# Down products by column quarters, four early blocks of the second input product, shared banks and a new place for memory blocks in a two-block decoder kernel

## Chip, cores and metric

The kernel runs on one core of one Trainium2 chip. The metric is the device time of one execution in microseconds; smaller is better. The weights lie in HBM and are read once.

## What is computed

Two decoder blocks over 256 tokens of width 1024, in fp32. The first ends in a mixture of 32 experts, of which each token takes two; the kernel reads all experts' weights. The second has four mixers on slices of one input product, a cross attention to 256 memory rows and a feed-forward net.

```python
hid = jax.nn.silu(jnp.matmul(xb, w_g[e])) * jnp.matmul(xb, w_u[e])
return jnp.matmul(hid, w_d[e]) * wb[:, None]
...
proj = rms_norm_2(h, g_mix[l]) @ w_in[l]
ya = short_conv_mixer(pa, w_sconv[l])
yb = dilated_mixer(pb, cos, sin)
yc = forgetting_mixer(pc, b_forget[l])
yd = pool_mixer(pd, w_pool[l], pool_scale[l])
h = h + jnp.concatenate([ya, yb, yc, yd], axis=-1) @ w_out[l]
h = h + memory_cross_attention(rms_norm_2(h, g_xa[l]), rms_norm_2(mem, g_mem[l]), w_xq[l], w_xkv[l], w_xo[l])
h = h + conv_ffn(rms_norm_2(h, g_ffn[l]), w_up[l], w_ffconv[l], w_down[l])
```

## The kernel before

**Weights** come as tiles of 1 MiB ([128 x 2048] fp32) into a ring of 23 slots in SBUF. `build` (L561 to L622) writes the order of all loads as a list, `coming`; `pump` issues the next one from SP (`load_next`, L326) when a slot is free. Dense weights are used as blocks of half a tile. Most are split into a high part (ACT, L369) and a low part (DVE, L372), and a product is then three products, L461 to L463 (`mm3`: low by high, high by low, high by high). A block in the list `FULL`, or an early block of `wkv`, is not split and is multiplied in fp32.

**Experts** (`experts`, L1428): eight groups of four experts. The four experts of a group stand side by side in the array, 32 rows each. A group has 16 tiles of gate and up weights (L1544) and 8 tiles of down weights (`down`, L1515). A down tile holds one 128-row slice f of the hidden width and one half n of the columns for the four experts: four products of 512 columns. After the eight tiles a half's sum is copied out (ACT), brought back to token order by products with `back` (L1597, called y here) and added to xT. For the last group this is `back_half`, started after four and after eight down tiles; it also makes the high and low parts (`norm_high`, `norm_low`) of xT for the second block's input product.

**Memory blocks** are the 16 blocks of `w_xkv`: eight of keys (L472) and eight of values (L1399 in fp32). Four are multiplied in block 1, eight at group 6 (`MOE_AT`, `MOE_KV`), three behind the last down tile (`V_PLACE`, split), and one among the mixers. `AHEAD_OF_LAST` puts one of their tiles in front of the last four expert tiles in the list of loads.

**The second block's input product**, columns for queries and keys (`pq`) and for values (`pv`): four blocks of two k-slices each (`projN`, L502), each 12 products of 512 columns. Both are made in `mixers`, first `pq`, then `pv`.

**Output products** use `partT` (L489): for the first `k` outputs (128 columns each) the k-slices already known are multiplied, and once attention is there the rest. In block 1 two outputs are made in this way, in the mixers' output three (`MIX_PART`), in cross attention four. Each output has a PSUM bank of its own. When an output is finished, `residual` adds it to xT on DVE (L1649; L1114 in block 1) and makes the norm pieces of the next stage.

**Order of work.** Each engine works in program order. The program is written as a main line with coroutines: `spawn` starts one, each `tick` lets each go one step. `horizon` limits how far ahead weight blocks may be split. In the feed-forward net the last four down blocks are multiplied at the end, first for the one, then for the other half of the columns (`products`, L2079).

Of the kernel before, what the change touches and what calls it, by code (L numbers as in the profile page):

```python
# [14 lines left out]
OP = mybir.AluOpType  # L15
# [3 lines left out]
P = 128  # L19
# [27 lines left out]
AHEAD_OF_LAST = (1, 4)  # L47
MEM_AT = 12
FILL = 1
MOE_KV = 8  # L50
MOE_AT = 6
RANK = 4
V_PLACE = 3
MIX_PART = 3
# [4 lines left out]
KV_EARLY = sum(KV_PLACE.values()) + MOE_KV  # L59
# [82 lines left out]
def pack(x):  # L142
# [8 lines left out]
    def chan(v):  # L151
# [38 lines left out]
    pa = blocks_T(w2[:, :768]).reshape(P, 3, 2, 1024).transpose(0, 2, 1, 3).reshape(P, -1)  # L190
    w2 = chunks(
        blocks_N(w2[:, 768:1280]), blocks_N(np.concatenate([w2[:, 1280:1536], w2[:, 2048:2304]], 1)),
# [6 lines left out]
    we = np.concatenate([four(eg, KT, 1), four(eu, KT, 1), four(ed, 4, 2)], 1)  # L199
# [35 lines left out]
class Net:  # L235
# [20 lines left out]
    def bank(self):  # L256
        return self.t(self.ps, [P, 512], "ps")

# [88 lines left out]
    def queue(self, name, shapes):  # L347

        n = len(shapes)
        return [  # L350
            ((name, j // 2), j % 2, s, j % 2 == 1 or j == n - 1, (name == "wkv" and j < KV_EARLY) or (name, j) in FULL) for j, s in enumerate(shapes)
        ]
# [112 lines left out]
    def projT(self, out, w, h, ks, col=0, start=None, stop=None):  # L465

        for k in ks:
# [3 lines left out]
            if len(w) == 1:  # L471
                self.nc.tensor.matmul(out, w[0][:, k, c], h[2][:, k, :], start=a, stop=z)  # L472
            else:
                self.mm3(out, (w[0][:, k, c], w[1][:, k, c]), (h[0][:, k, :], h[1][:, k, :]), a, z)
# [14 lines left out]
    def partT(self, outs, h, first, rest):  # L489

        ws = []
        for o in outs:
            ws.append(self.next_block())
            self.projT(o, ws[-1][0], h, first, stop=False)
            yield None
        self.before_rest()
        for i, (o, (w, release)) in enumerate(zip(outs, ws)):
            self.projT(o, w, h, rest, start=False)
            release()
            yield i  # L500

    def projN(self, outs, h):  # L502

        for b in range(4):
            w, release = self.next_block()
            for j in range(2):
                k = 2 * b + j
                for tt in range(2):
                    s = slice(tt * P, tt * P + P)
                    if len(w) == 1:  # L510
                        self.nc.tensor.matmul(outs[tt][:], h[2][:, k, s], w[0][:, j, :], start=k == 0, stop=k == 7)
                    else:
                        self.mm3(
                            outs[tt][:], (h[0][:, k, s], h[1][:, k, s]), (w[0][:, j, :], w[1][:, j, :]), k == 0, k == 7
                        )
            release()
# [44 lines left out]
    def build(self):  # L561
# [35 lines left out]
        late = KV_EARLY + V_PLACE  # L597
# [1594 lines left out]
```

## Time and profile before

| | |
|---|---|
| median of 3 runs | 1049.95 us (1049.3 to 1051.71) |
| profiled execution, its own time | 1052.21 us |
| its span in the profile | 1050.40 us |
| mean granted TensorE clock | 0.925 |
| busy: PE, DVE, ACT | 907.5, 515.6, 344.0 us |
| read by DMA | 301.61 MB |

The span is the profiled part of one execution. "Idle before" in a row is the time for which that engine stood still ahead of the instruction, with what released it. The clock is a share of 2.4 GHz. Matmuls overlap: a row's duration is longer than the distance to the next start.

### The profile page before, as it was taken

Reading aid. Unit: us, or ns where it says so; the run is one execution under the profiler, and the core shown is the slowest. Engines: PE = TensorE matmul, PEld = TensorE weight load, DVE = VectorE, ACT = ScalarE, POOL = GpSimd, SP = SyncE. Lnnn points to the kernel's source line nnn. Section 1 sums busy time; section 2 is a strip of 40 time slices with the busy share of each in tenths; the row PEclk is TensorE's granted clock in tenths of the full one; section 3 lists DMA queues with packets and bytes.
Section 4 is the critical chain, followed back from the end, with each engine's and each line's share of the span. In section 5 each row is a group of like instructions: output and inputs, shape, how many; then the busy total and the mean of one; then the engine's idle time right before and its main releaser. Section 6 shows DMA issues by size and latency. Waiting matters only on the chain.

```text
span 1050.4 us, 14787 instructions
## 1 busy us (share of the span) xinstructions
PE 907.5 (86%) x5988; PEld 641.7 (61%) x5989; DVE 515.6 (49%) x1133; ACT 344.0 (33%) x614; POOL 1.3 (0%) x12
## 2 busy tenths in 40 slices
PE   6999989979776667576865986999999999999996
PEld 6659979834312204031322621688899899999995
DVE  7999968521110101001010021648576489888886
ACT  5326645311100001000000011564464466555553
POOL 0000000000000000000000000000000000000000
PEclk9999999999976968889789996999999999999999
DMA  9926556879999999999999999952364285552001
GB/s 370 386 79 240 175 187 212 336 301 426 426 427 427 427 426 426 426 427 427 427 427 425 428 426 427 426 189 88 120 223 181 83 363 179 195 185 97 1 1 41
DMA packets 44778, 301.61 MB, mean 287 GB/s; under 512 B 5024, under 2 KB 7456, under 8 KB 8864
## 3 DMA queue, kind: packets, MB, share of 16 engines
q1 hardware_dynamic: 44128, 300.01, 70.8%
q8 instruction: 49, 0.80, 0.3%
q10 hardware_dynamic: 576, 0.59, 0.2%
q14 instruction: 25, 0.20, 0.1%
HBM read 299.54 MB, written 1.05 MB: 286 GB/s over the span
## 4 chain that ended last, share of the span: by engine, by line
DMA 38%; PE 37%; DVE 2%; ACT 1%; issue 0%; SPq 0%; ACTq 0%; DVEq 0%
DMA slot<-in_we_dram 36%; PE ps L461 10%; PE ps L463 10%; PE ps L462 10%; DMA slot<-in_wkv_dram 2%; PE ps L1515 1%; PE ps L1544 1%; DVE slot L372 1%; PE ps L1995 1%; PE ps L1961 1%; PE ps L1597 0%; PE ps L1490 0%; PE ps L1581 0%; PE ps L1777 0%; PE ps L1774 0%
## 5 line engine op out<-in xcount | busy, mean ns | idle before, releaser
L461 PE MATMUL ps<-slot,slot 128*128 128x256 f32 (+1 forms) x1020 | 304.3, 298 | 0.4 <-DVE k L1836 0.4
L462 PE MATMUL ps<-slot,slot 128*128 128x256 f32 (+1 forms) x1020 | 296.8, 291 | 0.9 <-DVE slot L372 0.8
L463 PE MATMUL ps<-slot,slot 128*128 128x256 f32 (+1 forms) x1020 | 296.8, 291 | 0.3 <-DVE slot L372 0.2
L1544 PE MATMUL ps<-slot,k 128*32 128x512 f32 x1024 | 163.7, 748 | 81.0 <-DMA slot<-in_we_dram 74.7
L461 PEld LDWEIGHTS ps<-slot,slot 128*128 128x128 f32 x1020 | 195.9, 192 | 12.3 <-issue 7.0
L462 PEld LDWEIGHTS ps<-slot,slot 128*128 128x128 f32 x1020 | 196.0, 192 | 6.1 <-DVE slot L372 1.8
L372 DVE TENSOR_TENSOR slot<-slot,slot 128x1024 fp32r<-128x1024 f32 x159 | 191.9, 1218 | 13.5 <-ACT slot L369 13.5
L463 PEld LDWEIGHTS ps<-slot,slot 128*128 128x128 f32 x1020 | 195.9, 192 | 3.3 <-DVE slot L372 0.7
L369 ACT ACTIVATE slot<-slot 128x1024 fp32r<-128x1024 f32 x158 | 163.6, 1050 | 48.4 <-PE ps L463 38.6
L1544 PEld LDWEIGHTS ps<-slot,k 128*32 128x32 f32 x1024 | 26.7, 119 | 210.1 <-DMA slot<-in_we_dram 164.2
L1515 PE MATMUL ps<-slot,k 128*32 128x512 f32 x512 | 68.8, 667 | 25.9 <-DMA slot<-in_we_dram 20.0
L1583 DVE TENSOR_TENSOR xT<-xT,ps 128x512 f32<-128x512 f32 x28 | 19.3, 688 | 115.9 <-PE ps L1581 115.9
L1552 DVE TENSOR_TENSOR k<-k,ps 128x512 f32<-128x512 f32 x8 | 5.5, 687 | 127.8 <-PE ps L1544 127.8
L1492 ACT ACTIVATE k<-ps 128x512 f32<-128x512 f32 x16 | 9.6, 597 | 160.2 <-PE ps L1490 160.2
L1551 DVE SCALAR_TENSOR_TENSOR k<-k,ps 128x512 f32<-128x512 f32 x8 | 5.5, 689 | 109.7 <-ACT k L1550 109.7
L1515 PEld LDWEIGHTS ps<-slot,k 128*32 128x32 f32 x512 | 14.4, 115 | 73.0 <-DMA slot<-in_we_dram 35.6
L722 DVE SCALAR_TENSOR_TENSOR slot<-slot,params,slot 128x256 f32<-128x256 f32 x120 | 51.6, 479 | 0.0
L1490 PEld LDWEIGHTS ps<-k,slot 128*128 128x128 f32 x256 | 36.1, 229 | 18.3 <-issue 16.3
L1490 PE MATMUL ps<-k,slot 128*128 128x128 f32 x256 | 37.6, 316 | 9.4 <-DVE k L1421 9.4
L1550 ACT ACTIVATE k<-ps 128x512 f32<-128x512 f32 x8 | 4.8, 597 | 121.8 <-PE ps L1544 113.6
L463 PE MATMUL ps<-slot,k 128*128 128x512 f32 (+1 forms) x96 | 36.6, 381 | 1.0 <-DVE k L2058 1.0
L1637 ACT ACTIVATE k<-k,params 128x256 f32<-128x256 f32 x46 | 21.0, 503 | 49.6 <-DVE k L2053 46.1
(343 smaller groups left out, 923.9 us busy)
## 6 DMA issues: line engine op xcount, KB each, us to landing
slot<-in_we_dram SPq DMA_DIRECT2D x192, 1024.0 KB, 19.6
slot<-in_w_dram SPq DMA_DIRECT2D x47, 1024.0 KB, 9.1
slot<-in_wup_dram SPq DMA_DIRECT2D x22, 1024.0 KB, 5.1
slot<-in_wdn_dram SPq DMA_DIRECT2D x11, 1024.0 KB, 4.9
slot<-in_wkv_dram SPq DMA_DIRECT2D x8, 1024.0 KB, 19.5
xT<-in_xT_dram SPq DMA_DIRECT2D x2, 512.0 KB, 4.9
slot<-in_w_dram SPq DMA_DIRECT2D x2, 512.0 KB, 6.5
slot<-in_mem_dram SPq DMA_DIRECT2D x1, 1024.0 KB, 4.9
```

The costliest lines, as they stand in the source:

```text
L369: self.nc.scalar.activation(hi, w, AF.Copy)
L372: self.nc.vector.tensor_tensor(lo, w, hi.bitcast(F32), OP.subtract)
L461: mm(out, l[0], r[0], start=start, stop=False, **kw)
L462: mm(out, l[0], r[1], start=False, stop=False, **kw)
L463: mm(out, l[1], r[0], start=False, stop=stop, **kw)
L722: stt(a, y[:, i, j : j + T], half_taps[:, i, j : j + 1], a, OP.mult, OP.add)
L1490: mm(pg[:, j * P : j * P + P], h2[:, tt, k * P : k * P + P], flat(oh, tt), start=tt == 0, stop=tt == 1)
L1515: mm(pd[n][32 * e : 32 * e + 32, :], hT[:, f * P + 32 * e : f * P + 32 * e + 32], t[:, 512 * e : 512 * e + 512], start=f == 0, stop=f == 3,)
L1544: mm(pgu[m][32 * e : 32 * e + 32, :], xg[k // 4][:, k % 4 * P + 32 * e : k % 4 * P + 32 * e + 32], t[:, 512 * e : 512 * e + 512], start=k ...
L1583: tt_(xflat[:, s], xflat[:, s], py[:], OP.add)
L1637: self.nc.scalar.activation(y, u, AF.Copy, scale=taps[:, 2:3])
L1961: mm(s[:, tt * T : tt * T + T], q[:, j * T + tt * P : j * T + tt * P + P], self.mk[:, 2 * hd + j, :], start=j == 0, stop=j == 1,)
```

## The change

Six things are edited.

1. **Down weights by quarters.** A down tile now holds a quarter of the columns (256) and two slices f for the four experts, so `down` makes eight products of 256 columns for a tile, and a quarter's sum is complete after two tiles. Two quarters share a bank. For the last group `back_quarter` runs after every second tile.
2. **Early blocks.** The first two blocks of `pq` and of `pv` (`EARLY = 2`) are multiplied inside the last group: `pq` block 0 after down tile 3, `pv` block 0 after tile 4, the blocks 1 after tile 7. Their two tiles are packed in turn and loaded ahead of the last group's down tiles.
3. **Memory blocks.** Two at group 4, eight at group 6, two among the mixers; all of them in fp32, without a split of the memory.
4. **Shared banks.** `partT`'s outputs lie two to a bank (`pairs`), in block 1, mixers and cross attention. `MIX_PART` is 6 instead of 3.
5. **Attention steps** of the mixers start one block later.
6. **The last down blocks of the feed-forward net** go block by block, both column halves of each.

```diff
-AHEAD_OF_LAST = (1, 4)
-MOE_KV = 8
-MOE_AT = 6
+MOE_KV = {4: 2, 6: 8}
+V_LAST = 2
-V_PLACE = 3
-MIX_PART = 3
+EARLY = 2
+MIX_PART = 6
...
+    def pairs(self, n):
+        banks = [self.bank() for _ in range((n + 1) // 2)]
+        return [banks[i // 2][:, i % 2 * T : i % 2 * T + T] for i in range(n)]
...
-        for o in outs:
+        for i, o in enumerate(outs):
             ws.append(self.next_block())
-            self.projT(o, ws[-1][0], h, first, stop=False)
+            self.projT(o, ws[-1][0], h, first, start=i % 2 == 0, stop=False, skip_group_check=True)
             yield None
...
-        late = KV_EARLY + V_PLACE
-        self.blocks += bm[at:late] + w2[:20] + bm[late:] + w2[20:]
+        self.blocks += bm[at:-V_LAST] + w2[:20] + bm[-V_LAST:] + w2[20:]
...
+        for g, e in enumerate(of_experts):
+            n = MOE_KV.get(g, 0) // 2
+            mixed += e[:16] + self.coming[at : at + n]
+            at += n
+            if g == 7:
+                mixed += self.coming[at : at + EARLY]
+                at += EARLY
+            mixed += e[16:]
...
         def down(g, j):
-            n, f = j // 4, j % 4
+            q = j // 2
             t = self.take(("e", g, 16 + j))
-            for e in range(4):
-                mm(
-                    pd[n][32 * e : 32 * e + 32, :], hT[:, f * P + 32 * e : f * P + 32 * e + 32],
-                    t[:, 512 * e : 512 * e + 512], start=f == 0, stop=f == 3,
-                )
+            for i in range(2):
+                f = 2 * (j % 2) + i
+                for e in range(4):
+                    mm(
+                        pd[q // 2][32 * e : 32 * e + 32, q % 2 * T : q % 2 * T + T],
+                        hT[:, f * P + 32 * e : f * P + 32 * e + 32], t[:, 1024 * i + T * e : 1024 * i + T * e + T],
+                        start=q % 2 + f == 0, stop=f == 3, skip_group_check=True,
+                    )
...
         for j in range(8):
             down(7, j)
+            if j == 7:
+                self.horizon = len(self.blocks)
+            self.tick()
+            if j % 2:
+                last = self.spawn(back_quarter(j // 2))
+                self.tick()
             if j == 3:
-                self.horizon = 2 * AHEAD_OF_LAST[0]
-                self.spawn(back_half(0))
-            self.tick()
-            if j >= 3:
-                self.fill_splits()
-        last = self.spawn(back_half(1))
-        for i in range(4 * V_PLACE):
-            next(self.kv)
-            self.tick()
+                early(self.pq, 0)
+            elif j == 4:
+                early(self.pv, 0)
+        early(self.pq, 1)
+        early(self.pv, 1)
         self.finish(last)
...
-        outs = [self.bank()[:, :T] for _ in range(k)]
+        outs = self.pairs(k)
...
-        for c in range(2):
-            two(0, c, 0, n)
+        for j in range(n):
+            for c in range(2):
+                two(0, c, j, j + 1)
```

What moves shows in the order of PE's instructions. "Waits" names the engine whose semaphore the instruction waits for; line numbers of the changed kernel are 8 to 15 higher (L469 to L471 are the three split products, L1524 the down product, L1602 y, L1660 the residual add, L1130 that of block 1, L1414 the value product).

The first place is PE at the rest products of block 1's two partial outputs. Before:

```order
L461 MATMUL ps_1879<-slot_232_1822,slot_228_1759 128x256 [waits Activation_49]
L462 MATMUL ps_1879<-slot_232_1822,slot_228_1759 128x256 [waits DVE_49]
L463 MATMUL ps_1879<-slot_232_1822,slot_228_1759 128x256
L461 MATMUL ps_1880<-slot_232_1822,slot_230_1795 128x256
L462 MATMUL ps_1880<-slot_232_1822,slot_230_1795 128x256
L463 MATMUL ps_1880<-slot_232_1822,slot_230_1795 128x256
...
L461 MATMUL ps_1942<-slot_224_1719,slot_234_1834 128x256
```

and with the change:

```order
L469 MATMUL ps_1879<-slot_232_1822,slot_228_1759 128x256 [waits Activation_49]
L470 MATMUL ps_1879<-slot_232_1822,slot_228_1759 128x256 [waits DVE_49]
L471 MATMUL ps_1879<-slot_232_1822,slot_228_1759 128x256
L469 MATMUL ps_1879<-slot_232_1822,slot_230_1795 128x256 [waits DVE_49]
L470 MATMUL ps_1879<-slot_232_1822,slot_230_1795 128x256
L471 MATMUL ps_1879<-slot_232_1822,slot_230_1795 128x256
...
L469 MATMUL ps_1941<-slot_224_1719,slot_234_1834 128x256
```

The two outputs, ps_1879 and ps_1880 before, are one bank, ps_1879, after; the first rest product of the second output now waits for DVE.

The second place is PE at the rest products of the mixers' output with the change (ps_5440 and ps_5441 are banks of two outputs each; each output's rest has twelve products, of which the first three stand here):

```order
L469 MATMUL ps_5440<-slot_722_4947,slot_779_5326 128x256
L470 MATMUL ps_5440<-slot_723_4948,slot_779_5326 128x256
L471 MATMUL ps_5440<-slot_722_4947,slot_779_5326 128x256
...
L469 MATMUL ps_5440<-slot_722_4947,slot_784_5369 128x256 [waits DVE_49]
L470 MATMUL ps_5440<-slot_723_4948,slot_784_5369 128x256
...
L469 MATMUL ps_5441<-slot_722_4947,slot_793_5411 128x256
L470 MATMUL ps_5441<-slot_723_4948,slot_793_5411 128x256
...
L469 MATMUL ps_5441<-slot_722_4947,slot_805_5444 128x256 [waits DVE_49]
L470 MATMUL ps_5441<-slot_723_4948,slot_805_5444 128x256
```

Every second output of a bank begins with a wait for DVE; before there are three outputs in three banks here, and no such wait.

The third place is PE at the last four down tiles. Before (ps_4211, ps_4212 the two halves, ps_4244 to ps_4301 y, ps_4288 and ps_4289 memory values):

```order
L1515 MATMUL ps_4212<-slot_637_4150,k_648_4209 32x512 x4
L1597 MATMUL ps_4244<-k_598_3948,k_656_4234 128x256 x2
L1597 MATMUL ps_4247<-k_598_3948,k_656_4234 128x256 x2
L1515 MATMUL ps_4212<-slot_638_4156,k_648_4209 32x512 x4
L1515 MATMUL ps_4212<-slot_639_4162,k_648_4209 32x512 x4
L1515 MATMUL ps_4212<-slot_640_4168,k_648_4209 32x512 x4
L461 MATMUL ps_4288<-slot_657_4236,slot_612_4024 128x512
L462 MATMUL ps_4288<-slot_657_4236,slot_612_4024 128x512
L463 MATMUL ps_4288<-slot_657_4236,slot_613_4025 128x512
L461 MATMUL ps_4289<-slot_657_4236,slot_612_4024 128x512
```

and with the change (ps_4463, ps_4464 are `pq`, ps_4465, ps_4466 `pv`, ps_4444 and ps_4445 the down sums):

```order
L1524 MATMUL ps_4444<-slot_637_4383,k_648_4442 32x256 x8
L469 MATMUL ps_4463<-slot_656_4451,slot_651_4446 128x512
L470 MATMUL ps_4463<-slot_656_4451,slot_651_4446 128x512
...
L1602 MATMUL ps_4527<-k_599_4167,k_667_4513 128x256 x2
L1524 MATMUL ps_4445<-slot_638_4389,k_648_4442 32x256 x8
L469 MATMUL ps_4465<-slot_657_4453,slot_651_4446 128x512
...
L1524 MATMUL ps_4445<-slot_639_4395,k_648_4442 32x256 x8
L1524 MATMUL ps_4445<-slot_640_4401,k_648_4442 32x256 x8
L1602 MATMUL ps_4583<-k_599_4167,k_672_4571 128x256 x2
L1524 MATMUL ps_4445<-slot_641_4407,k_648_4442 32x256 x8
L469 MATMUL ps_4463<-slot_658_4455,slot_651_4446 128x512
...
L1602 MATMUL ps_4625<-k_599_4167,k_678_4607 128x256 x2
L469 MATMUL ps_4465<-slot_659_4457,slot_651_4446 128x512
```

Blocks of the input product, 12 products each, stand between the down tiles where before the down tiles follow one another, and behind the last one the blocks 1 of `pq` and `pv` come in the place of memory values.

## Rows read from the trace of the kernel before

**Rows 1.** Page, part 4: the chain that ended last, shares by line.
```profile
DMA slot<-in_we_dram 36%; PE ps L461 10%; PE ps L463 10%; PE ps L462 10%; DMA slot<-in_wkv_dram 2%; PE ps L1515 1%; PE ps L1544 1%; DVE slot L372 1%; PE ps L1995 1%; PE ps L1961 1%; PE ps L1597 0%; PE ps L1490 0%; PE ps L1581 0%; PE ps L1777 0%; PE ps L1774 0%
```

**Rows 2.** Busy us (instructions) of each engine, PEclk, DMA share, GB/s, by stretch.
```profile
222.00:662.65 440.65, 325.05 (x1992) 120.20 (x1991) 46.91 (x88) 39.66 (x73) 0.00 (x0) 0.84 1.01 427
662.65:1043.00 380.35, 376.38 (x2630) 346.46 (x2626) 283.51 (x550) 199.36 (x340) 0.69 (x5) 1.00 0.42 155
```

**Rows 3.** PE waits from 655 us: waiter, releaser, us in total, times, longest.
```profile
PE ps L1515 <- DMA slot<-in_we_dram: 3.7, 1, 3.7
...
PE ps L463 <- DVE k L2058: 1.0, 1, 1.0
```

**Rows 4.** Page, part 6: issues of expert tiles, KB, us to landing.
```profile
slot<-in_we_dram SPq DMA_DIRECT2D x192, 1024.0 KB, 19.6
```

**Rows 5.** Timeline at the last expert tiles: start us, us, engine, line.
```profile
655.37 1.93 PE L1515 MATMUL ps<-slot,k 128*32 128x512 f32 x8 [3.65 <-DMA slot<-in_we_dram]
657.24 3.78 PE L1597 MATMUL ps<-k,k 128*128 128x256 f32 x8
660.95 2.88 PE L1515 MATMUL ps<-slot,k 128*32 128x512 f32 x24
...
662.65 0.28 PEld L1515 LDWEIGHTS ps<-slot,k 128*32 128x32 f32 x8 [0.58 <-DMA slot<-in_we_dram]
```

**Rows 6.** Timeline of PE, 692 to 701 us; groups, 662.65 to 701.3 us.
```profile
692.13 1.03 PE L1703 MATMUL ps<-ident,slot 128*128 128x128 f32 x8
...
692.92 0.48 PE L461 MATMUL ps<-slot,slot 128*128 128x512 f32 x1
...
695.75 0.28 PE L461 MATMUL ps<-slot,k 128*8 128x256 f32 x1
...
698.49 0.40 PE L461 MATMUL ps<-slot,slot 128*128 128x512 f32 x1
...
701.01 0.39 PE L463 MATMUL ps<-slot,slot 128*128 128x512 f32 x1
...
L461 PE MATMUL ps<-slot,slot 128*128 128x512 f32 x44 | 17.8, 405 | 0.0
...
L445 PE MATMUL ps<-k,ones 128*128 128x256 f32 x2 | 0.6, 378 | 0.0
```

**Rows 7.** Value product: duration ns min/median/max, first and last start us.
```profile
L1399 PE MATMUL ps<-slot,slot x32: 592/592/592, 591.0 to 604.3; 128*128 128x512 f32 x32
```

**Rows 8.** Timeline, 722 to 723 us, DVE and PE.
```profile
722.53 0.41 DVE L1836 TENSOR_TENSOR k<-ps,rb 128x256 f32<-128x256 f32 x1
...
723.09 0.36 PE L461 MATMUL ps<-slot,slot 128*128 128x256 f32 x1 [0.42 <-DVE k L1836]
```

**Rows 9.** Timeline, 778 us: residual adds beside PE.
```profile
778.65 0.28 PE L463 MATMUL ps<-slot,slot 128*128 128x256 f32 x1
...
778.77 0.28 PE L461 MATMUL ps<-slot,slot 128*128 128x256 f32 x1
...
778.97 0.42 DVE L1649 TENSOR_TENSOR xT<-ps,xT 128x256 f32<-128x256 f32 x1 [0.59 <-PE ps L463]
```

**Rows 10.** Timeline of DVE in the cross attention's output.
```profile
840.00 0.42 DVE L1649 TENSOR_TENSOR xT<-ps,xT 128x256 f32<-128x256 f32 x1
...
841.73 0.42 DVE L1649 TENSOR_TENSOR xT<-ps,xT 128x256 f32<-128x256 f32 x1
```

**Rows 11.** Timeline in block 1, 179 to 181 us.
```profile
178.98 2.35 DVE L372 TENSOR_TENSOR slot<-slot,slot 128x1024 fp32r<-128x1024 f32 x2
...
179.45 0.28 PE L461 MATMUL ps<-slot,slot 128*128 128x256 f32 x1
...
181.25 0.75 DVE L1114 SCALAR_TENSOR_TENSOR xT<-ps,xT 128x256 f32<-128x256 f32 x2
```

**Rows 12.** Busy time by stretch, before the expert stream.
```profile
215.00:220.00 5.00, 4.31 (x42) 2.27 (x44) 0.29 (x1) 0.60 (x1) 0.00 (x0) 1.00 0.14 56
```

**Rows 13.** Busy time by stretch, a dip of the granted clock.
```profile
728.00:733.00 5.00, 5.00 (x23) 4.34 (x24) 4.68 (x15) 0.91 (x5) 0.00 (x0) 0.66 0.47 192
```

More of the change, by code (lines that the diff above doesn't have):

```diff
@@ L58 @@
 ACT_EVERY = 2
-KV_EARLY = sum(KV_PLACE.values()) + MOE_KV
 LAM_INIT = 0.8 - 0.6 * math.exp(-0.3 * 0)
@@ L350, in queue @@
         return [
-            ((name, j // 2), j % 2, s, j % 2 == 1 or j == n - 1, (name == "wkv" and j < KV_EARLY) or (name, j) in FULL) for j, s in enumerate(shapes)
+            ((name, j // 2), j % 2, s, j % 2 == 1 or j == n - 1, name == "wkv" or (name, j) in FULL) for j, s in enumerate(shapes)
         ]
@@ L497, in partT, with block_N @@
         for i, (o, (w, release)) in enumerate(zip(outs, ws)):
-            self.projT(o, w, h, rest, start=False)
+            self.projT(o, w, h, rest, start=False, skip_group_check=True)
             release()
             yield i
+    def block_N(self, outs, h, b):
+        w, release = self.next_block()
+        for j in range(2):
+            k = 2 * b + j
+            for tt in range(2):
+                s = slice(tt * P, tt * P + P)
+                if len(w) == 1:
+                    self.nc.tensor.matmul(outs[tt][:], h[2][:, k, s], w[0][:, j, :], start=k == 0, stop=k == 7)
+                else:
+                    self.mm3(
+                        outs[tt][:], (h[0][:, k, s], h[1][:, k, s]), (w[0][:, j, :], w[1][:, j, :]), k == 0, k == 7
+                    )
+        release()
     def projN(self, outs, h):
         for b in range(4):
[L505 to L514, printed above, removed]
-                        )
-            release()
+            self.block_N(outs, h, b)
             yield
@@ L1128, in residual @@
             mm(pl[:36, :T], wr[:, i, :], hg[:, i, :], start=i == 0, stop=end)
-        outs = []
-        for i in range(2):
-            b = self.bank()
-            outs.append(b[:, :T])
+        outs = self.pairs(2)
         for i in self.partT(outs, m_hl, range(6), range(6, 8)):
@@ L1292, in overflow_expert @@
                 for f in range(4):
-                    wd = load(16 + 4 * half + f, ks[2 + f % 2])
+                    wd = ks[2 + f % 2]
+                    for q in range(2):
+                        src = self.io["we"][ds(g, 1), 16 + 4 * half + 2 * q + f // 2, :, ds(1024 * (f % 2) + 256 * e, 256)]
+                        nc.sync.dma_start(wd[:, q * T : q * T + T], src.rearrange("o p c -> p (o c)"))
                     for i in range(4):
@@ L1564, in experts @@
                 break
-            if g == MOE_AT:
-                for _ in range(4 * MOE_KV):
-                    next(self.kv)
-                    self.tick()
-                self.memory_split()
+            for _ in range(4 * MOE_KV.get(g, 0)):
+                next(self.kv)
+                self.tick()
             if g == 1:
@@ L1605, in back_half, with early @@
                 self.norm_high(n2, xT[:, k, :], k)
-            for k in ks:
+            for k in (2 * q, 2 * q + 1):
                 self.norm_low(n2, xT[:, k, :], k)
+        self.horizon = 2 * EARLY
+        self.fill_splits()
+        self.fill_splits()
+        self.pq, self.pv = [[self.bank(), self.bank()] for _ in range(2)]
+        def early(outs, b):
+            self.block_N(outs, n2.h, b)
+            self.tick()
         for j in range(8):
             down(7, j)
-            if j == 3:
-                self.horizon = 2 * AHEAD_OF_LAST[0]
-                self.spawn(back_half(0))
@@ L1708, in rotary @@
                 act(qkT[:, :, tt * P : tt * P + P], pts[tt][:].rearrange("p (j t) -> p j t", j=4), AF.Copy)
-        pq = [self.bank(), self.bank()]
-        for b, _ in enumerate(self.projN(pq, h)):
+        pq, pv = self.pq, self.pv
+        for b in range(EARLY, 4):
+            self.block_N(pq, h, b)
             if b == 3:
@@ L1714, in mixers @@
             self.tick()
-        pv = [self.bank(), self.bank()]
         def keep_v():
```

91 lines of the change are left out of this document (38 added, 53 removed).

## Prediction

> **What bounds the kernel now.** I read the chain of waits first: 36% of the span is the arrival of expert tiles, and 30% PE's split products, L461 to L463 [rows 1]. Busy time by stretch says when: from 222 to 662.65 us the DMA share is 1.01, and from 662.65 to 1043 us PE is busy 376.38 of 380.35 us [rows 2]. Of PE's waits behind 655 us two of the three longest matter here: 3.7 us ahead of the last down tiles, 1.0 near the end [rows 3]. So work in front of 662.65 is free while PE is ahead of DMA, a tile added to that stream costs its transfer, and work or a wait of PE behind it costs its full length.
>
> Sums are made against the profiled execution (1052.21 us, span 1050.40). The median of the runs shown, 1049.95, lies 2.26 below it. About 0.2%, 2.1 us, is what a measurement of this kernel can tell from no change.
>
> **The hand-off from DMA to PE.** Each 1 MiB expert tile takes 19.6 us from issue to landing [rows 4] with eight in flight, so one lands every 19.6 / 8 = 2.45 us. The loop that orders the loads now puts five wkv tiles among or ahead of the 192 expert tiles; after, five of wkv and two of w2. Two more tiles move the last landing by **+4.9 us**.
>
> Now PE's weight load waits for the last tile until 662.65 [rows 5]. The last value product begins at 701.01 and makes room 0.2 later: 38.6 us. In it stand eight rotary transposes (692.13 to 692.92, 0.8) and 24 forget products (695.75 to 698.49, 2.7) that come behind the value products in the changed order, so the like stretch is 35.0. It holds 132 split products of 512 columns, three lines of 44, 96 of them w2 and 36 wkv [rows 6].
>
> After the change, twelve such products make a block. Those from 698.49 to 701.01 are 2.52 / 11 = 0.229 apart [rows 6], so a block is 2.73 us. Six blocks remain behind the last down tile: 16.4. Two products of y at a quarter of 1.89, the half-time of the eight at 657.24 [rows 5], 0.47; statistics and spread 0.6, as the spreads' row has it [rows 6]; 0.2 for changes of operand. Together 17.65.
>
> Between the landing and the end of the last down products it depends on TensorE's clock. Eight down products took 1.93 us at 655.37, and 24 took 2.88 at 660.95, 0.96 for eight [rows 5]: both levels, 1.2 and 2.4 GHz, stand within 6 us. PE has four down tiles, y and two early blocks to do in the four last tile times, 4 x 0.96 + 0.9 + 5.5 = 10.2 against 9.8, so it is some 0.5 late; with the last tile (1.0), y (0.5) and the wait's lag it is done 2.2 us behind the landing at the higher level. At the lower level for the last early block and the last tile, 2.73 + 0.96 more: 5.9. I take 3.7, nearer to the first, since early blocks keep PE at work where it now stands idle. The hand-off: 4.9 + 3.7 + 17.65 - 35.0 = **-8.8 us** (-10.3 to -6.6).
>
> Covered by the 2.45 us of each tile and thus nothing: down products of half the width and twice the number (even 1.2 instead of 0.96 us a tile), quarters in place of halves on ACT and DVE, the memory split that goes away, and two more value blocks in fp32 (7 us, below). If that cover were gone, the last would cost its 7 us.
>
> **The value blocks left.** Among the mixers one split block was left, 2.73 us; now two are, in fp32. Four blocks of 32 products span 591.0 to 604.9 [rows 7], 3.48 each, so 6.95. PE is full there: **+4.2 us**.
>
> **The end.** The last down products go pair by pair, both column halves of a pair together, so the product that stands idle for DVE's L2058 [rows 3] has others in front of it: **-0.9 us** (0 to -1.2).
>
> **The shared banks** are the term against the change. The order shows a wait on DVE at the first rest product of each odd output: three in the mixers' output, two in the cross attention's, one in block 1. An add on DVE must have read the first half of the bank. Before, each output has its own bank and no such wait. The price shows once in the trace of before, where a product into the second half of a bank stands behind L1836, which reads the first: L1836 starts at 722.53, takes 0.41, and the product starts at 723.09, 0.15 later [rows 8]. The add of L1649 starts at 778.97, 0.20 behind the first product of the next output (778.77), and takes 0.42, on a DVE that was idle [rows 9]. A wait costs 0.20 + 0.42 + 0.15 = 0.77 at least.
>
> In the mixers' output a rest is twelve products, 0.12 apart [rows 9], 1.44 us; in cross attention six, 0.72. Between two adds DVE has two norm instructions and waits for ACT: 1.73 from 840.00 to 841.73 [rows 10]. In the mixers' output each later add comes 1.73 - 1.44 = 0.29 late: 0.77 + 1.06 + 1.06 = 2.9. In cross attention the second is 1.73 - 0.72 = 1.01 late: 0.77 + 1.78 = 2.55. In block 1 the next output's product would start at 179.45, but DVE is in two splits until 181.25 and then adds for 0.42 [rows 11]: 181.67 + 0.15 - 179.45 = 2.37. That stall lies ahead of the DMA stretch and passes on: at 215 to 220 us the DMA share is 0.14 [rows 12], its slots full and waiting for PE. Together **+7.8 us**: 4.6 if all six are at the floor, 10 if splits stand in front of more of them.
>
> The Trainium skill speaks against this edit. "Perfetto Trace Analysis", section "Optimizing Tensor Performance", wants independent groups of products to rotate through different banks, so that the emptying of one overlaps the next group's products. "PSUM — Partial Sum Buffer", section "PSUM bank collisions raise a hardware error", guards a bank, not an address: by address alone no wait would be needed and the sum would be 7.8 lower, 1044.4; by bank it is the sum below. The trace agrees with the bank: [rows 8] show the wait, 0.42, for another half.
>
> **Other moves.** The clock granted from 728 to 733 us is 0.66 [rows 13], of 5 us some 1.7 lost; it may go, or come elsewhere: -1.7 to +1.7, taken as 0. Attention starts a block later but now has six first parts (6 x 1.44 = 8.6 us) in front of the rest that needs it, instead of three: 0. On SP the two w2 loads go ahead of the last eight expert tiles, which is the 4.9 above, and nothing else that PE waits for stands behind them.
>
> **Sum:** -8.8 + 4.2 - 0.9 + 7.8 = **+2.3 us**, 1054.5 against 1052.21; against the median 1052.2.
>
> **Rivals.** (a) *DVE is ahead.* A waiting PE lets DVE empty its queue: each add is at its floor, and block 1 gets its stall back, as DVE's splits are then done early and the following products wait for none. Five waits remain, 3.85 us: -8.8 + 4.2 - 0.9 + 3.85 = -1.65, or -3.15 with the clock at 2.4 GHz at the hand-off: 1048.3 to 1046.8. For it: DVE was idle in front of the add at 778.97 [rows 9]. Against: it sat in two splits at 178.98 [rows 11]. It decides where the waits add up to less than 5 us. (b) *Slow clock, full DVE.* 1.2 GHz through the last tiles, +2.2, and three waits of 1.78 among the mixers, +2.4: +6.9, 1056.9. For it: 1.93 us at 655.37 [rows 5]; against: PE has more to do there than now. (c) *The change doesn't do what it says.* If the first quarters are late, the two early blocks run behind the last tile, 5.5 more: 1057.7. Against: the first two quarters are whole four tiles, 9.8 us, ahead of the end.
>
> **How the numbers follow.** Forecast 0.45 (0.02 faster, 0.23 same, 0.20 slower); (a) 0.33 (0.24 faster, 0.09 same); (b) 0.14 and (c) 0.08, slower. Faster 0.26, same 0.32, slower 0.42. The range goes from 1045.5, (a) with most of the dip at 728 us gone as well, to 1057.0, just past (b). The forecast's own is 1049.5 to 1054.5.
>
> **What would show it.** The last expert tile lands some 7 us later than now (4.9 and block 1's 2.4), and from there to the last value product it is 21 to 22 us. The list of PE's waits has the mixers' and cross attention's add (L1660 after the change) with five waits of 0.8 to 1.8 us, and the add of block 1 (L1130) with one of some 2.4. Products of L1414 stand behind the hand-off for 7 us, and no wait near the end. I am wrong if the hand-off doesn't shorten, if such waits don't appear, or if the stream doesn't move with block 1.

## The result and the profile after

The change takes 1060.22 us (median of 4 runs, 1059.77 to 1060.72) against 1049.72 for the kernel before: a ratio of 1.0096, 95% interval 1.0079 to 1.0114. That is 10.5 us slower, where the forecast was 2.3 slower and the range ended at 1057.0. The profiled execution took 1060.72 us with a span of 1059.0, 8.6 more than the span before; the ledger below is made of these two spans.

The chain of waits of the changed kernel, with the same parts as before [rows 1]; new in it are the memory blocks' products (L1414 values, L480 keys) and the residual add (L1660):

```profile
DMA slot<-in_we_dram 33%; PE ps L469 10%; PE ps L471 10%; PE ps L470 10%; PE ps L1414 3%; DMA slot<-in_wkv_dram 2%; PE ps L1524 1%; PE ps L1554 1%; PE ps L2010 1%; PE ps L1976 1%; PE ps L480 1%; PE ps L1496 1%; PE ps L1602 0%; DVE xT L1660 0%; PE ps L1789 0%
```

PE's waits of the changed kernel from 640 us on (waiter, releaser, us in total, times, longest), to be read beside [rows 3]:

```profile
PE ps L469 <- DVE k L1849: 4.7, 1, 4.7
PE ps L469 <- DVE xT L1660: 4.2, 5, 1.5
PE ps L1524 <- ACT slot L377: 3.5, 1, 3.5
...
PE ps L2010 <- ACT k L2004: 1.5, 2, 0.7
PE ps L471 <- DVE slot L380: 1.4, 1, 1.4
PE ps L1567 <- DVE k L1562: 0.8, 1, 0.8
PE ps L1524 <- ACT k L1598: 0.6, 1, 0.6
```

The five waits on the residual add were forecast. The largest, 4.7 us for L1849, and the 1.4 us for a weight split (L380) were not. L1849 is the line that was L1836 before, where it held PE for 0.42 us [rows 8]. At that place the kernel before had no wait for a weight split. The wait of 3.5 us for L377 stands at the first of the last down tiles, where the expert stream still sets the pace: PE waits for DMA again at each of the next three (0.48, 0.85 and 0.17 us).

In PE's timeline of the changed kernel the same waits have their places (start, us, line; in brackets the idle time before):

```profile
177.14 0.28 PE L471 MATMUL ps<-slot,slot 128*128 128x256 f32 x1
179.53 0.39 PE L469 MATMUL ps<-slot,slot 128*128 128x256 f32 x1 [2.10 <-DVE xT L1130]
179.75 0.28 PE L470 MATMUL ps<-slot,slot 128*128 128x256 f32 x1
...
218.86 3.64 PE L1554 MATMUL ps<-slot,k 128*32 128x512 f32 x32 [0.69 <-ACT k L1498]
...
671.60 1.07 PE L1524 MATMUL ps<-slot,k 128*32 128x256 f32 x16
...
690.91 1.04 PE L1714 MATMUL ps<-ident,slot 128*128 128x128 f32 x8
...
717.77 0.56 PE L469 MATMUL ps<-slot,slot 128*128 128x256 f32 x1 [4.69 <-DVE k L1849]
...
777.45 0.39 PE L469 MATMUL ps<-slot,slot 128*128 128x256 f32 x1 [0.52 <-DVE xT L1660]
...
781.39 0.39 PE L469 MATMUL ps<-slot,slot 128*128 128x256 f32 x1 [0.81 <-DVE xT L1660]
...
785.35 0.39 PE L469 MATMUL ps<-slot,slot 128*128 128x256 f32 x1 [0.82 <-DVE xT L1660]
...
791.57 0.39 PE L471 MATMUL ps<-slot,slot 128*128 128x256 f32 x1 [1.41 <-DVE slot L380]
...
845.97 0.39 PE L469 MATMUL ps<-slot,slot 128*128 128x256 f32 x1 [0.52 <-DVE xT L1660]
...
849.20 0.38 PE L469 MATMUL ps<-slot,slot 128*128 128x256 f32 x1 [1.54 <-DVE xT L1660]
...
864.42 0.50 PE L433 MATMUL ps<-ones,sq_sum 128*128 128x1 f32 x4
```

A wait costs more than the idle time in the brackets. From 177.14 to 179.75 us there are 2.61 us where two products at 0.12 us would take 0.24: 2.37 us are lost with 2.10 of idle, as the last product in front and the first one behind the wait take longer than the distance between products. By the starts around them the waits on L1660 lose 0.78, 1.08 and 1.08 us among the mixers and 0.78 and 1.80 in cross attention, and the one on L380 loses 1.68.

The marks of the kernel before on PE that answer to those, from its timeline:

```profile
217.22 3.64 PE L1544 MATMUL ps<-slot,k 128*32 128x512 f32 x32 [0.69 <-ACT k L1492]
...
763.29 1.25 PE L1918 MATMUL ps<-ident,k 128*128 128x128 f32 x8 [0.34 <-DVE k L1910]
...
824.04 1.99 PE L1995 MATMUL ps<-k,slot 128*128 128x256 f32 x8 [0.74 <-ACT k L1989]
...
854.96 0.50 PE L425 MATMUL ps<-ones,sq_sum 128*128 128x1 f32 x4
```

And the expert loads' last issues in SP's queue, of the changed kernel:

```profile
636.92 12.54 SPq L334 DMA_DIRECT2D slot<-in_we_dram  x6
```

The last issue of these six lies 0.33 us before 636.92 + 12.54 = 649.46, at 649.13. The last eight expert loads take 19.5 to 19.6 us to land; with 19.55 it is 668.7. The stretches between these marks make the ledger (the attended transposes of the changed kernel start at 763.26, its first cross attention value product at 830.94):

| stretch | before, us | after, us | difference | forecast |
|---|---|---|---|---|
| to the first expert product | 217.22 | 218.86 | +1.6 | +2.4 |
| to the last expert tile's landing | 445.4 | 449.8 | +4.4 | +4.9 |
| to the end of the value products (before: less 3.5 for work placed later) | 35.0 | 22.2 | -12.8 | -13.7 |
| to the attended transposes (before: with those 3.5) | 65.6 | 72.4 | +6.8 | part of +4.2 |
| to the cross attention's first value product | 60.75 | 67.68 | +6.9 | +2.9 and the rest of +4.2 |
| to the feed-forward norm's statistics | 30.9 | 33.5 | +2.6 | +2.55 |
| to the end | 195.4 | 194.6 | -0.9 | -0.9 |

Five stretches came out within 0.9 us of the forecast. The two in the middle, the mixers, were forecast at 7.1 together and took 13.7. A second profile of the change (run a0, below) has 448.2 us to the last landing and 23.9 from there to the end of the value products; the hand-off as a whole comes out the same, 8.3 us gained where the table has 8.4, but the single rows move by up to 1.7 us between executions.

### The profile page after: what moved, and what is told of

Same layout as the page of the kernel before. It is cut to its first block, busy times and chain, and to the rows that moved or that the text cites. A ratio compares the mean times of both kernels' runs of the same rounds, so it can differ in the third digit from the quotient of the medians.

```text
span 1059.0 us, 15764 instructions
## 1 busy us (share of the span) xinstructions
PE 914.0 (86%) x6484; PEld 656.8 (62%) x6485; DVE 509.7 (48%) x1125; ACT 338.1 (32%) x608; POOL 1.3 (0%) x12
## 4 chain that ended last, share of the span: by engine, by line
PE 39%; DMA 35%; DVE 2%; ACT 1%; issue 0%; SPq 0%; ACTq 0%; DVEq 0%
DMA slot<-in_we_dram 33%; PE ps L469 10%; PE ps L471 10%; PE ps L470 10%; PE ps L1414 3%; DMA slot<-in_wkv_dram 2%; PE ps L1524 1%; PE ps L1554 1%; PE ps L2010 1%; PE ps L1976 1%; PE ps L480 1%; PE ps L1496 1%; PE ps L1602 0%; DVE xT L1660 0%; PE ps L1789 0%
## 5 line engine op out<-in xcount | busy, mean ns | idle before, releaser
L469 PE MATMUL ps<-slot,slot 128*128 128x256 f32 (+1 forms) x1004 | 299.9, 299 | 11.1 <-DVE k L1849 4.7
L471 PE MATMUL ps<-slot,slot 128*128 128x256 f32 (+1 forms) x1004 | 291.6, 290 | 1.6 <-DVE slot L380 1.6
L470 PE MATMUL ps<-slot,slot 128*128 128x256 f32 (+1 forms) x1004 | 291.5, 290 | 0.1
L1554 PE MATMUL ps<-slot,k 128*32 128x512 f32 x1024 | 169.4, 772 | 74.5 <-DMA slot<-in_we_dram 69.0
L469 PEld LDWEIGHTS ps<-slot,slot 128*128 128x128 f32 x1004 | 193.9, 193 | 24.3 <-issue 12.4
L470 PEld LDWEIGHTS ps<-slot,slot 128*128 128x128 f32 x1004 | 194.0, 193 | 4.7 <-DVE slot L380 0.7
L471 PEld LDWEIGHTS ps<-slot,slot 128*128 128x128 f32 x1004 | 193.9, 193 | 4.3 <-DVE slot L380 2.0
L380 DVE TENSOR_TENSOR slot<-slot,slot 128x1024 fp32r<-128x1024 f32 x155 | 186.9, 1218 | 6.5 <-ACT slot L377 6.5
L377 ACT ACTIVATE slot<-slot 128x1024 fp32r<-128x1024 f32 x154 | 159.1, 1049 | 33.3 <-PE ps L471 23.6
L1554 PEld LDWEIGHTS ps<-slot,k 128*32 128x32 f32 x1024 | 26.9, 121 | 207.7 <-DMA slot<-in_we_dram 162.4
L1524 PE MATMUL ps<-slot,k 128*32 128x256 f32 x1024 | 66.3, 404 | 23.7 <-DMA slot<-in_we_dram 15.3
L1524 PEld LDWEIGHTS ps<-slot,k 128*32 128x32 f32 x1024 | 31.7, 114 | 56.0 <-DMA slot<-in_we_dram 21.4
L469 PE MATMUL ps<-slot,k 128*128 128x512 f32 (+1 forms) x96 | 36.9, 384 | 0.0
## 6 DMA issues: line engine op xcount, KB each, us to landing
slot<-in_we_dram SPq DMA_DIRECT2D x192, 1024.0 KB, 19.6
slot<-in_wkv_dram SPq DMA_DIRECT2D x8, 1024.0 KB, 19.5
```

The costliest lines, as they stand in the source:

```text
L377: self.nc.scalar.activation(hi, w, AF.Copy)
L380: self.nc.vector.tensor_tensor(lo, w, hi.bitcast(F32), OP.subtract)
L469: mm(out, l[0], r[0], start=start, stop=False, **kw)
L470: mm(out, l[0], r[1], start=False, stop=False, **kw)
L471: mm(out, l[1], r[0], start=False, stop=stop, **kw)
L1524: mm(pd[q // 2][32 * e : 32 * e + 32, q % 2 * T : q % 2 * T + T], hT[:, f * P + 32 * e : f * P + 32 * e + 32], t[:, 1024 * i + T * e : 102 ...
```

## The experiments

Twelve runs were made, in three groups of four (e, then a0 and c, then d), each group on one chip with the kernel before beside it; the times are compared as ratios to that. Two executions of one kernel differ by up to 6.6 us (29 runs of the kernel before: 1045.86 to 1052.43). Between the profiles the start of the expert stream moves by 2.3 us and its length by 2.8, so a part of the program is also compared by its stretch in the trace: from the last down tile's first product to the attended transposes (M1, 91.7 us in the change), from there to the cross attention's first value product (M2, 67.7), from there to the statistics (M3, 33.5). M2 and M3 repeat within 0.04 us where an edit leaves them alone. M1 does not: in the six profiles whose edits do not touch it (the change, a0, d1, d2, e3, e4) it lies between 90.3 and 93.1 us.

The change itself has two ratios, 1.0096 in the result above and 1.0119 in run a0, on different chips, and it did not run beside the e and d groups. The gains given below for e1 to e4 are against 1.0096, those for the d runs of the change against 1.0119; against the other value they would be 2.4 us larger or smaller. For a single edit the stretches therefore say more than the times.

**Is the 4.7 us the latency of the forget gates' chain?** In the changed kernel DVE's queue ahead of L1849 reads like this (timeline of DVE):

```profile
708.70 0.40 DVE L1761 SCALAR_TENSOR_TENSOR slot<-slot 8x256 f32<-8x256 f32 x1
710.92 0.41 DVE L1765 TENSOR_TENSOR slot<-slot 8x256 f32<-8x256 f32 x1 [1.82 <-ACT slot L1764]
...
712.33 0.68 DVE L1770 TENSOR_TENSOR_SCAN slot<-slot 8x256 f32<-8x256 f32 x1
713.05 0.40 DVE L1772 TENSOR_SCALAR slot<-slot,consts 8x256 f32<-8x256 f32 x1
713.37 1.48 DVE L1774 TENSOR_SCALAR slot<-slot,consts 8x256 f32<-8x256 f32 x4
714.78 1.21 DVE L380 TENSOR_TENSOR slot<-slot,slot 128x1024 fp32r<-128x1024 f32 x1
...
717.21 0.42 DVE L1849 TENSOR_TENSOR k<-ps,rb 128x256 f32<-128x256 f32 x1
```

L1761 to L1774 are the forget gates. The line `self.finish(fg)` puts all that is left of them in DVE's queue ahead of the pool mixer, then come a weight split and two attention steps, then L1849. PE was done with its last work in front of the pool mixer's second product at 713.08.

Run e1 starts the forget gates earlier:

```diff
-        for b in range(EARLY, 4):
-            self.block_N(pq, h, b)
-            if b == 3:
-                rope = self.spawn(rotary(pq))
-            self.tick()
...
         for b in range(EARLY, 4):
-            self.block_N(pv, h, b)
+            self.block_N(pq, h, b)
+            if b == 3:
+                rope = self.spawn(rotary(pq))
             if b == EARLY:
                 fg = self.spawn(forget())
+            self.tick()
+
+        for b in range(EARLY, 4):
+            self.block_N(pv, h, b)
```

> The change, with the forget gates' products moved from behind the first query-key block of the forgetting mixer to between the last two value blocks, some 5.7 us of PE work earlier. Theory A: PE's 4.7 us wait for the pool mixer's L1849 is the latency of the forget chain (17 us on DVE and ACT), which the order puts in DVE's queue ahead of that instruction; then the wait falls under 0.5 us, the half clock behind it (0.76 granted from 718 to 730 us) goes as well, and the run is 4 to 6.5 us faster than the change, about 1054 to 1056. Theory B: DVE is simply full there (90% busy); then the wait reappears within the next blocks and the run gains under 1.5 us.

Measured: 1058.78 us, ratio 1.0096 (1.0073 to 1.0118), no gain that the times show. M1 is 90.05, 1.6 shorter than in the change's first profile and just below the 90.3 to 93.1 of the others, so it shows no gain for certain either. PE's waits of this run in the mixers:

```profile
PE ps L469 <- DVE xT L1660: 2.2, 3, 0.8
PE ps L469 <- DVE k L1850: 2.0, 1, 2.0
PE ps L471 <- DVE slot L380: 1.4, 1, 1.4
PE ps L469 <- DVE slot L1836: 0.5, 1, 0.5
```

The wait fell from 4.7 to 2.0 and a new one of 0.5 came. So the forget chain is part of it but not the whole: its steps come one at each tick of the main line and stand behind instructions that wait for PE's next block, so an earlier start of its products moved L1849 (here L1850) by 2.0 us only, from 45.6 to 43.7 us behind the last down tile's first product. Theory A, as stated, fell. Theory B's small gain is what came, but that DVE is simply full is not what the rows of the change show: it stands idle for 1.82 us inside the forget chain, waiting for ACT (L1764).

**Is it the shared bank that hands DVE's lateness to PE?** Run e2 gives the pool mixer's two products a bank each:

```diff
-            if i % 2 == 0:
-                pp = self.bank()
-            o = pp[:, i * T : i * T + T]
+            o = self.bank()[:, :T]
```

> The change, with the pool mixer's two products in banks of their own instead of two halves of one. Theory A (a shared bank is what hands DVE's lateness to PE): the 4.7 us wait for L1849 goes and PE runs on at full clock, 4 to 6.5 us faster than the change. Theory B (DVE and ACT are late anyway): PE waits as long a little later, at the short convolution's products or ahead of the attended transposes, and the run gains under 2 us.

Measured: 1057.56 us, ratio 1.0075 (1.0048 to 1.0101), 2.2 us less than the change by the ratio; M1 is 86.9, 4.8 shorter, and 3.4 below the lowest of the six that leave it alone. The wait is gone and only 0.6 us for ACT comes instead:

```profile
PE ps L469 <- DVE xT L1660: 4.2, 5, 1.5
PE ps L2008 <- ACT k L2002: 1.5, 2, 0.7
PE ps L471 <- DVE slot L380: 1.4, 1, 1.4
PE ps L1868 <- ACT k L1813: 0.6, 1, 0.6
```

By its trace theory A holds in its main point: DVE and ACT were no later than PE could bear; only the bank made PE wait for them. Two parts of it did not come: the time gained is below the 4 to 6.5 us (against 1.0119 it would be 4.6), and PE did not run on at full clock (0.75 and 0.91 from 720 to 730 us, see the end).

**The partial products' banks.** Run e3 undoes `pairs` in the mixers' and the cross attention's output, with three first parts as before:

```diff
-MIX_PART = 6
+MIX_PART = 3
...
-        outs = self.pairs(k)
+        outs = [self.bank()[:, :T] for _ in range(k)]
```

> The change, with every output of the mixers' and the cross attention's partial products in a bank of its own, and three first parts among the mixers instead of six. Theory A (the shared banks cost what the trace shows): the five waits on the residual add, 4.2 us and some 0.15 us of restart each, go, and the run is 4 to 5.5 us faster than the change. Rival: the six first parts were the cover for attention; with three, PE waits 2 to 4 us for the attended rows instead, and the gain is under 2.5 us.

Measured: 1055.43 us, ratio 1.0059 (1.0035 to 1.0082), 3.9 us less than the change by the ratio. M2 is 63.11 (-4.6), M3 30.91 (-2.6), together 7.1. PE's list has no wait for the residual add, none for the attended rows and none for L380:

```profile
PE ps L469 <- DVE k L1849: 4.7, 1, 4.7
PE ps L2010 <- ACT k L2004: 1.5, 2, 0.7
```

So six first parts were not needed as cover. This run changes two things at once, the banks and the number of first parts; that the six parts brought the wait for L380 is seen in run d1, below.

Run d2 undoes the sharing in the cross attention alone:

```diff
-        outs = self.pairs(k)
+        outs = [self.bank()[:, :T] for _ in range(k)] if gname == "g_ffn2" else self.pairs(k)
```

> The change with own banks in the cross attention's output alone. Theory A: the two waits there (0.52 and 1.54 us, with restarts 2.4) go and nothing else changes: 2 to 2.8 us less than the change, ratio about 1.0095. Rival: DVE, a full period behind, hands its lateness to the feed-forward net's first blocks; under 1 us.

Measured: 1059.53 us, ratio 1.0087 (1.0061 to 1.0112) where the change had 1.0119; M3 is 30.91, 2.6 shorter, and M2 unchanged (67.67). The time gained is 3.4 us against a0's ratio and 0.9 against the first, so the stretch, not the time, carries theory A.

Run d1 keeps the shared banks, with three first parts:

```diff
-MIX_PART = 6
+MIX_PART = 3
```

> The change with three first parts among the mixers instead of six, banks still shared. Theory A: only one odd output is left, so one wait of 0.5 us on L1660 instead of three (2.15 us), and the 1.4 us wait for a weight split (L380) behind the six goes, as six blocks' high and low parts no longer fill the ring of slots: 3 to 4 us less than the change (ratio to before about 1.008 where the change had 1.0119). Rival: six parts were needed as cover; then PE waits for the attended rows ahead of the rests, and the run is not faster than the change.

Measured: 1059.09 us, ratio 1.0095 (1.0069 to 1.0120), and M2 63.88, 3.8 shorter. One wait of 0.52 us is left there, and L380 no longer holds PE: two waits on L1660 at 1.08 us each and 1.68 for L380 make the 3.8. So of the 4.6 us that run e3 takes off M2, 3.8 come with the six parts and 0.8 with the one shared bank that is left. Whether six parts with a bank each would still wait for L380 was not run.

**Block 1.** Run e4 undoes the sharing there:

```diff
-        outs = self.pairs(2)
+        outs = [self.bank()[:, :T] for _ in range(2)]
```

> The change, with block 1's two partial outputs in banks of their own. Theory A (a stall ahead of the expert stream passes through to the end one to one): the wait of 2.1 us on L1130 goes, the last expert tiles come about 2.1 us earlier and the run is 1.7 to 2.5 us faster than the change. Rival: the routing or the free slots set the stream's start, and the run is within 0.7 us of the change.

Measured: 1057.86 us, ratio 1.0097 (1.0072 to 1.0122), no gain in the times. In its trace the wait of 2.1 us is gone and the first expert product starts at 215.16. In the seven profiles of the changed kernel and its variants with that shared bank this start lies between 218.86 and 221.17, in the six with own banks there (this one and the five below that have own banks throughout) between 215.16 and 216.99. So the stall does pass to the start of the stream; that it comes out at the end one to one is not shown by this run alone. (Against 1.0119 the times would show 2.3 us.)

**All of it together.** Run c1 has the edits of e2, e3 (with its three first parts) and e4, and nothing else; run a0 is the change once more on the same chip.

> The change itself once more, on the chip of the next three runs, so that they can be compared with it: 1.008 to 1.011 times the kernel before. Its trace should again show 4.7 us for L1849, five waits on L1660 and one on L1130.

> The change with all its shared halves undone: own banks in block 1, in the mixers' output (three first parts), in the cross attention's and for the pool mixer's two products. Theory A (each wait for a half of a bank costs its length at the end, one to one): from the three single traces 2.1 + 6.5 + 4.9 = 13.5 us less than the change, so 3 us faster than the kernel before (ratio 0.997, 0.995 to 1.000). Rival (PE runs into DVE's lateness elsewhere, or the single gains are one gain): 5 to 8 us less than the change, so still 2 to 5 us slower than before.

Measured: the change 1060.61 us, ratio 1.0119 (1.0097 to 1.0141); own banks 1045.13 us, ratio 0.9963 (0.9947 to 0.9978). The ratios are 0.0156 apart, 16 us; the expected sum was 13.5. This kernel is faster than both, 3.7 us less than the one before beside it (1048.82). PE's waits of this run from 640 us on:

```profile
PE ps L1524 <- ACT slot L377: 3.6, 1, 3.6
PE ps L1554 <- DMA slot<-in_we_dram: 2.8, 2, 1.4
PE ps L2008 <- ACT k L2002: 1.5, 2, 0.7
PE ps L1868 <- ACT k L1813: 1.2, 1, 1.2
```

Nothing that was taken away came back elsewhere, apart from 1.2 us for ACT. M1 to M3 are 86.0, 63.1 and 30.9. Theory A holds: the waits that the single traces show add up. The times of the single runs do not say so by themselves: against 1.0096 e2, e3 and e4 gain 6 us together, against 1.0119 some 13.

Run c2 adds e1's earlier forget gates to c1:

> The kernel of own banks, with the forget gates' products between the last two value blocks as well. Theory A (no wait is left for DVE where the forget chain stood, so its start no longer matters): within 1 us of the run with own banks. Rival (the forget chain still holds back the attention steps): 1 to 3 us faster than that run.

Measured: 1045.91 us, ratio 0.9975 (0.9962 to 0.9989), within 1.3 us of own banks and inside its interval. With own banks no effect of the forget gates' place can be told from the spread.

**The price of the memory blocks.** Run c3 leaves four value blocks among the mixers instead of two:

```diff
-MOE_KV = {4: 2, 6: 8}
-V_LAST = 2
+MOE_KV = {6: 8}
+V_LAST = 4
```

> The kernel of own banks, with two memory value blocks more left among the mixers (four instead of two) and one memory tile less among the experts. By the prediction's prices: 2 x 3.48 = 6.95 us more of PE behind the hand-off, 2.45 us less ahead of it: 4.5 us slower than the run with own banks. Rival (PE has idle time among the mixers, waiting for attention, which the blocks fill): under 2 us slower.

Measured: 1050.33 us, ratio 1.0006 (0.9991 to 1.0022), 4.5 us over own banks by the ratio, as expected. M2 is 69.97, 6.9 longer, against 2 x 3.48 = 6.95.

**The attention's start.** Run d3 is c1 with the attention steps one block earlier, as in the kernel before:

```diff
             if b == 3:
                 self.after(0, keep_v)
+                self.finish(rope)
+                heads = [self.spawn(attend(0, 0))]
             self.tick()
-        heads = []
...
-            if j:
-                self.finish(rope)
-                heads.append(self.spawn(attend(0, j - 1)))
+            if j < 3:
+                heads.append(self.spawn(attend(0, j + 1)))
```

The five steps behind these move up by one block in the same way.

> The kernel of own banks, with the attention steps started as in the kernel before, one block earlier. The prediction priced this move at nothing: within 1 us of the run with own banks (ratio 0.9963). Rival: the later start is what keeps DVE clear for the blocks behind it, and the earlier start costs 1 to 3 us.

Measured: 1048.00 us, ratio 0.9994 (0.9977 to 1.0011), 3 us over own banks by the ratio, with intervals that just touch. Its profile shows less: M1 85.6 and M2 64.0, together 0.5 longer than in c1, with one new wait, 1.6 us for the forget gates (L1774). So the later start is no loss and may be a gain; how large stays open.

**The early blocks.** Run d4 is c1 with the first two blocks moved behind the last down tile:

```diff
-            if j == 3:
-                early(self.pq, 0)
-            elif j == 4:
-                early(self.pv, 0)
+        early(self.pq, 0)
+        early(self.pv, 0)
         early(self.pq, 1)
```

> The kernel of own banks, with the two early blocks 0 of the input product moved behind the last down tile. Theory A: 2 x 2.73 us of products leave the time of the expert stream; PE was some 2 us late at the last tile with them, so 3 to 5.5 us slower than the run with own banks, and up to 2 more if TensorE's clock is at 1.2 GHz at the last tile as in the kernel before. Rival: the last tiles leave PE no room and the early blocks only changed places with the tiles; under 1 us.

Measured: 1046.90 us, ratio 0.9976 (0.9962 to 0.9990), 1.3 us over own banks, between the two theories. Its trace around the last down tile, on PE, and its last expert loads on SP:

```profile
663.53 1.07 PE L1524 MATMUL ps<-slot,k 128*32 128x256 f32 x16 [1.60 <-ACT k L1598]
664.54 1.13 PE L1602 MATMUL ps<-k,k 128*128 128x256 f32 x4
665.60 1.07 PE L1524 MATMUL ps<-slot,k 128*32 128x256 f32 x16
...
636.11 10.08 SPq L334 DMA_DIRECT2D slot<-in_we_dram  x5
```

The last load is issued at 636.11 + 10.08 - 0.33 = 645.86 and lands at 665.4; the last down tile's first product starts at 665.60. With the early blocks it starts 2.9 us behind the landing in the change (671.60 against 668.7) and 3.5 in c1. Two blocks are 5.5 us, of which some 3 come back as lateness at the last tile. The 2 to 3 us that are left are more than the 1.3 measured, but within the two intervals (0.9947 to 0.9978 and 0.9962 to 0.9990).

## Why the prediction was wrong

- **Hand-off: right in sum.** Tile landing +4.4 (forecast 4.9), and 22.2 us from there to the end of the value products (21.35): together -8.4 against -8.8. The last tile's products began 2.9 us behind the landing and end about one us later, close to the 3.7 taken. But the slow clock that was half assumed for it did not come: the last tile's down products took 1.07 us, near the 0.96 of the upper of the two levels [rows 5], with 1.00 granted from 670 to 675 us. At that level the forecast had 2.2. PE was later because the early blocks did not fit beside the tiles, with a wait of 0.56 for ACT's copy of a quarter; without them (run d4) it starts 0.2 us behind the landing. That 3.7 came close to the measured 3.9 is luck.
- **Memory blocks: right.** +4.2 was forecast; run c3 measured two further blocks at 6.9 us of PE, and 4.5 net of a tile.
- **End: right**, -0.9 in the last stretch, and no wait near the end is left.
- **Shared banks: right where they were counted, within 0.05 us.** By what each wait loses, block 1 lost 2.37 us (2.37 forecast), the mixers' three waits 0.78, 1.08 and 1.08, together 2.9 (2.9), and cross attention 2.6 (2.55). Only the block 1 term came out smaller at the start of the stream, +1.6, where that start moves by 2 us between profiles. The forecast's "order shows a wait on DVE at the first rest product of each odd output" counted only banks that the change newly shares. The Trainium skill's advice in "Perfetto Trace Analysis", section "Optimizing Tensor Performance", to rotate independent groups of products through different banks, is borne out: run c1, which does that and goes back to three first parts, is at 0.9963 where the change is at 1.0119.
- **The step that failed** is in what the forecast put at nothing among the mixers: the sentence on other moves, that six first parts with a later attention start cost 0, and the silent assumption that a gain of 8.8 us at the hand-off goes through the mixers whole. Two terms are missing. First, the pool mixer's two products share a bank already before; [rows 8] show that wait at 0.42 us, and the forecast read it only as a price for others. Now PE is ready for the second product 9.6 us earlier (713.08 instead of 723.09 - 0.42 = 722.67), but DVE reaches the instruction that must have read the first only 5.3 us earlier (717.21 instead of 722.53), with the forget gates' chain in front of it. The difference, 4.3, is what the wait grew by, from 0.42 to 4.69. Run e2 takes away the bank, and with it the wait; run e1, which starts the forget gates earlier, takes away 2.7 of it and adds 0.5 elsewhere. Second, with six first parts the next weight split comes late, and PE loses 1.7 us (1.41 of idle) that it does not lose with three (runs e3 and d1). That the six blocks' high and low parts fill the ring of slots is the likely reason, but not shown. Of the later attention start by itself no cost is shown (run d3). 4.3 + 1.7 are 6.0 of the 6.6 us by which the mixers' two stretches missed. Most of the rest is a longer stretch of lower clock: the 24 products behind L1849 took 5.5 us, the slowest block before 4.6, a block at the upper level 3.1.
- **The size of the miss.** Between the profiled executions it is 6.2 us (8.5 against 2.3); against the median it is 8.0, and the 2 us beyond are spread: the profiled execution before lay 2.5 us above the median, that of the change 0.5. None of the forecast's three signs of being wrong came: the hand-off shortened, the waits appeared and the stream moved with block 1. The largest part of the miss lay in a wait for which it had named no sign.
- **Rivals.** None of the three came. (a) expected every add at its floor and block 1's stall gone. The first wait among the mixers and the first in cross attention were at that floor (0.78 us lost, 0.77 forecast), but the later ones lost up to 1.80, and block 1's stall stayed. (b) put the loss on the clock at the last tiles, which ran at the upper level, and on mixers' waits of 1.78, which lost 0.78 to 1.08. (c) did not happen: the early blocks ran early.

## What to carry to other kernels

When work ahead of an engine is removed, follow the time saved to the next instruction that waits for another engine: a wait of 0.4 us there says that the slack is used up, and the gain ends at it unless the other engine's work moves too. A buffer shared by two independent results makes its writer wait for its reader, and turns all the reader's lateness into idle time of the writer; count the old shared buffers as well as the new. Here undoing the sharing, with three first parts instead of six, turned 11.8 us lost (run a0) into 3.7 us won (run c1).

## What the runs showed of the hardware that was not expected

- The stretch of lower clock behind 715 us is not simply PE's wait, and it is not bound to one place. Granted clock by 5 us: the change has 0.68 and 0.63 from 715 to 725 us, with 2.8 us of idle in the first. All seven profiles with the wait for the pool mixer's bank (a0, d1, d2, e1, e3, e4 and the change) have such a stretch right behind it. But run e2, without that wait, has 0.75 and 0.91 from 720 to 730, the kernel before 0.71 from 730 to 735, and run c2 0.91 and 0.75 from 740 to 750, with PE busy throughout; a0 has a second one, 0.75 and 0.91 from 745 to 755; and runs c1 and d3 have none, 1.00 from 670 to 860 us. What brings it stays open. The blocks of 24 products named above took 4.6 and 5.5 us in it and 3.1 outside, so it makes part of the spread of M1. Stretches of runs e2, c1 and c2, in this order (us, busy us and instructions of PE, PEld, DVE, ACT and POOL, granted clock, DMA share, GB/s):

```profile
720.00:725.00 5.00, 5.00 (x25) 4.10 (x25) 4.76 (x19) 2.58 (x6) 0.26 (x1) 0.75 0.49 156
...
720.00:725.00 5.00, 5.00 (x32) 3.54 (x31) 4.66 (x18) 2.54 (x5) 0.00 (x0) 1.00 0.48 185
...
745.00:750.00 5.00, 5.00 (x29) 4.48 (x29) 1.85 (x4) 1.39 (x5) 0.00 (x0) 0.75 0.00 2
```

- The expert stream has two lengths. From the first expert product to the last landing, worked out from the last issue as above, the profiles with the change's tiles have 448.1 to 448.4 us (seven) or 449.8 to 450.9 (five), on average 2.2 apart, about one tile (2.45). The change's own two profiles show both, 449.8 and 448.2, so this is spread between executions.
